# One load of a batched q k^T kernel, issued as nine partial transfers instead of one

## The chip, the core and the metric

The kernel runs on one core of a Trainium2 chip. The core has engines that run side by side, each with an instruction queue of its own: TensorE for matrix products (PE in the profile; PEld is its weight load), VectorE (DVE), ScalarE (ACT), GpSimd (POOL) and SyncE (SP), which only issues transfers and waits. Transfers between the chip's memory and the on-chip memory SBUF are done by 16 DMA engines, which ACT and SP feed through a queue each. SBUF has 128 partitions.

The metric is the device time of the program in microseconds. The time before is the median of three runs, 1063.87 us (1062.1 to 1064.1).

## The reference

```python
def setup_inputs():
    batch, n_heads, seq, head_dim = 8, 12, 1024, 64
    return {"q": ..., "k": ...}     # float32, (8, 12, 1024, 64) each

def reference(q, k):
    return np.einsum('bhid,bhjd->bhij', q, k).astype(np.float32)
```

For each of the 96 pairs of batch and head (called heads below) the scores are the 1024 x 1024 products of q's and k's rows. The inputs are 2 x 25 MB; the output is 96 x 4 MB, 403 MB.

## The kernel before

The 96 heads are grouped into nine blocks of 2, 2, 4, 8, 16, 16, 16, 16 and 16 heads (`sizes`). The first three blocks are small, so that work starts early, and block 3 (`EARLY`) is the first that is read into the input tile `x_sb`.

**Path of a block's inputs.** A block's q, and then its k, is read from memory as float32 into `x_sb`, each of the 128 partitions holding R = 8 N rows of 64 values for N heads. With 16 heads that is 8192 values, 32 KB, per partition and 4 MB in all. The method `load` does it with one transfer. `x_sb` has room for one such tensor, so a load first waits (`input_busy`) until the previous tensor has been read out. From there POOL casts it to 16 bits in pieces (`cast_quads`, line 210): a tensor of 16 heads has four pieces, each of four casts of 32 partitions. Every cast waits for the load's landing, `self.landed[x]`, which is a list of all landings of the tensor. The pieces lie in a ring of three buffers (`half`), from which DVE transposes them in 32 x 32 blocks (`transpose_quads`, line 229) into `qT` and `kT`, laid out as the products need them. Two sets of `qT` and `kT` alternate between blocks. Blocks 0 and 1 go another way, by PE's transposes.

**Scores of a head.** In `scores`, PE loads 128 columns of `qT` as weights (line 308) and multiplies with two halves of `kT` (line 311). Eight such row tiles make a head. Two of them fill half of PSUM (128 x 2048 float32), and ACT copies that half to an output tile (line 288), four copies for a head. The output tiles `o_sb` are a ring of three, 4 MB each. When a head's copies are done, SP issues one transfer of 4 MB for it (line 301); the tile is reused three heads later, when that store has landed.

**Order.** The instructions of each engine follow the order in which the program emits them. `block` runs over the heads of a block and hangs side work on them: during the heads of block i, the tensors of block i + 1 are loaded, cast and transposed. Loads are issued on ACT's queue, by `next_load(act)`, as side work of heads 1 and 7 of a block (after the copy of its second pair of row tiles): q of the next block at head 1, k at head 7. The transposes of the next block are emitted at heads 3 to 6 for q and 10 to 13 for k (`TURNS`). The last load of all is thus k of block 8 (heads 80 to 95), emitted at head 7 of block 7, head 71 of the whole.

**Landings.** A `Landing` is a semaphore that a transfer raises by 16 when it has landed. All loads of k into `x_sb` share one, and a wait names the count that it must have reached. `start` adds 16 for each transfer and returns the count up to which it has landed.

Of the kernel before, what the change touches and what calls it, by code (L numbers as in the profile page):

```python
# [8 lines left out]
P = 128  # L9
# [50 lines left out]
def kernel(  # L60
# [76 lines left out]
    class Block:  # L137
# [14 lines left out]
        def load(self, x, eng, landing=None):  # L152
            events = []
            if self.raw[x] is None:
                at = x * self.elems if self.i == EARLY else 0
                self.raw[x] = x_sb[:, at : at + self.elems]
                landing = input_landing[x]
                events = list(input_busy)
            src = flat[x][self.first * S : (self.first + self.N) * S]
            eng.wait(events)  # L160
            dma = eng.eng.dma_start(
                out=self.raw[x], in_=src.rearrange("(p r) d -> p (r d)", p=P)
            )
            self.landed[x].append(landing.start(dma))

        def load_head(self, n, x, eng, landing):
            start = (self.first + n) * S
# [156 lines left out]
    blocks, first = [], 0  # L324
# [31 lines left out]
    for x in range(2):  # L356
# [7 lines left out]
                out=ident,  # L364
                in_=ident,
# [100 lines left out]
```

## Time and profile before

| | |
|---|---|
| median of three runs | 1063.87 us (1062.1 to 1064.1) |
| profiled execution, its own time | 1062.84 us |
| its span, first to last instruction | 1061.0 us |
| TensorE clock granted | 1.0 |
| bytes moved | read 50.33 MB, written 402.65 MB |
| mean rate over the span | 427 GB/s |
| store of a head: 96 transfers on SP's queue | 4 MB each, 21.8 us from issue to landing (median) |
| load of a 16-head tensor: 10 transfers on ACT's queue | 4 MB each, 24.1 us (q) and 24.3 us (k) |
| copy of PSUM to the output tile, ACT line 288 | 384, mean 1859 ns |
| cast of 32 partitions x 2048, POOL line 210 | 176, mean 1888 ns |
| transpose, DVE line 229 | 44 of a 16- or 8-head tensor's pieces, mean 9478 and 9539 ns |

The span is the profiler's time from the first to the last instruction; the execution's own time has 1.8 us around it. Besides the engines' busy times, the profile has a record of every packet that a DMA engine moved, with its start, size and duration, and of every count by which a transfer's landing raised its semaphore: sixteen for each transfer. The packet records carry no engine number. They can be put into sixteen lanes, since on a full engine each packet begins where another ended.

A busy share of the DMA engines is the mean over the sixteen. A share slightly above 1 comes from packets that are counted whole in the window that they are assigned to.

### The profile page before, as it was taken

What the parts mean: (1) busy time and instruction counts of PE and PEld (TensorE: products, weight loads), DVE (VectorE), ACT (ScalarE), POOL (GpSimd) and SP (SyncE); (2) the same over time, 40 slices, a digit from 0 to 9 for tenths busy, and PEclk for the clock granted to TensorE, in tenths of its full rate; (3) what the DMA queues carried; (4) which work ended last, traced back from release to release, by engine and by line L of the source; (5) the groups of instructions that cost most, each with busy time, mean ns of one, the idle gap of its engine ahead of it and who ended that gap; (6) DMA issues with size and microseconds to landing.
All of it is one profiled execution on the core that took longest, in us unless ns stands there. A gap on an engine that the chain in (4) does not pass through costs nothing.

```text
span 1061.0 us, 3307 instructions
## 1 busy us (share of the span) xinstructions
PE 700.2 (66%) x1568; PEld 127.3 (12%) x800; DVE 431.0 (41%) x55; ACT 697.1 (66%) x386; POOL 354.2 (33%) x206
## 2 busy tenths in 40 slices
PE   6876744957477748567765856775584777778770
PEld 1111100111011101011111101111110111111110
DVE  2995939029193009339003907600761920000000
ACT  4766655857477747567756756775675777777771
POOL 7927465056380028064006509100913700000000
DMA  9999999999999999999999999999999999999997
GB/s 376 434 435 435 434 434 434 416 421 432 431 434 434 435 429 428 426 435 432 432 422 434 435 427 433 433 434 423 433 429 432 435 434 431 434 434 431 432 431 322
DMA packets 17009, 453.21 MB, mean 427 GB/s; under 512 B 1888, under 2 KB 1888, under 8 KB 2912
## 3 DMA queue, kind: packets, MB, share of 16 engines
q1 hardware_dynamic: 14976, 410.00, 89.7%
q10 hardware_dynamic: 2016, 42.99, 9.8%
q8 instruction: 9, 0.15, 0.0%
q14 instruction: 8, 0.07, 0.0%
HBM read 50.33 MB, written 402.65 MB: 427 GB/s over the span
## 4 chain that ended last, share of the span: by engine, by line
DMA 65%; ACT 16%; PE 7%; DVE 5%; POOL 4%; issue 1%; ACTq 0%; SPq 0%
DMA out_dram<-o_sb 60%; ACT o_sb L288 16%; PE ps_all L311 7%; DVE kT L229 4%; POOL half L210 3%; DMA x_sb<-in_k_dram 2%; DMA x_sb<-in_q_dram 2%; DVE qT L229 1%; DMA o_sb<-in_q_dram 0%; PE ps_all L243 0%; POOL qT L181 0%; DVE kT L250 0%; ACT kT L250 0%; ACTq L36 0%; SPq L169 0%
## 5 line engine op out<-in xcount | busy, mean ns | idle before, releaser
L288 ACT COPY o_sb<-ps_all 128x2048 f32<-128x2048 f32 (+1 forms) x384 | 694.8, 1859 | 333.5 <-DMA out_dram<-o_sb 290.2
L311 PE MATMUL ps_all<-kT,qT 64*128 64x512 f16 x1536 | 696.1, 617 | 328.6 <-ACT o_sb L288 312.8
L210 POOL CAST half<-x_sb 32x2048 f16<-32x2048 f32 x176 | 332.3, 1888 | 482.1 <-DMA x_sb<-in_q_dram 302.2
L229 DVE STREAM_TRANSPOSE qT<-half 128x2048 f16<-128x2048 f16 x22 | 202.6, 9478 | 268.1 <-POOL half L210 268.1
L229 DVE STREAM_TRANSPOSE kT<-half 128x2048 f16<-128x2048 f16 x22 | 202.5, 9539 | 137.5 <-POOL half L210 137.5
L308 PEld LDWEIGHTS <-qT 64*128 64x128 f16 x768 | 124.2, 162 | 897.4 <-issue 878.0
L229 DVE STREAM_TRANSPOSE kT<-kT 128x1024 f16<-128x1024 f16 x2 | 9.4, 4870 | 0.0
L229 DVE STREAM_TRANSPOSE qT<-qT 128x1024 f16<-128x1024 f16 x2 | 9.2, 4780 | 0.0
L210 POOL CAST qT<-o_sb 32x1024 f16<-32x1024 f32 x8 | 8.3, 1035 | 1.2 <-DMA o_sb<-in_q_dram 0.8
L210 POOL CAST kT<-o_sb 32x1024 f16<-32x1024 f32 x8 | 8.3, 1035 | 0.5
L250 DVE COPY qT<-ps_all 128x1024 f16<-128x1024 f16 x2 | 2.4, 1224 | 11.1 <-PE ps_all L243 11.1
L288 DVE COPY o_sb<-ps_all 128x1024 f32<-128x1024 f32 x4 | 4.9, 1225 | 4.4 <-PE ps_all L311 4.4
L243 PE MATMUL ps_all<-ident,qT 128*128 128x128 f16 x16 | 2.1, 311 | 6.8 <-POOL qT L181 6.7
L250 ACT COPY kT<-ps_all 128x1024 f16<-128x1024 f16 x1 | 1.0, 1012 | 4.8 <-PE ps_all L243 4.8
L181 POOL CAST qT<-o_sb 128x512 f16<-128x512 f32 x4 | 2.3, 615 | 3.7 <-DMA o_sb<-in_q_dram 3.7
L250 ACT ACT_TABLE_LOAD x1 | 1.3, 1283 | 2.8 <-issue 2.8
L250 DVE COPY kT<-ps_all 128x1024 f16<-128x1024 f16 x1 | 1.2, 1225 | 4.4 <-PE ps_all L243 4.4
L243 PE MATMUL ps_all<-ident,kT 128*128 128x128 f16 x16 | 2.0, 305 | 0.7 <-ACT o_sb L288 0.7
L181 POOL CAST kT<-o_sb 128x512 f16<-128x512 f32 x4 | 2.4, 618 | 0.3 <-DMA o_sb<-in_q_dram 0.3
L243 PEld LDWEIGHTS ps_all<-ident,qT 128*128 128x128 f16 x16 | 1.5, 141 | 7.1 <-POOL qT L181 7.1
L243 PEld LDWEIGHTS ps_all<-ident,kT 128*128 128x128 f16 x16 | 1.5, 136 | 3.3 <-POOL qT L210 1.6
L359 POOL MEMSET ident<- 128x128 f16 x1 | 0.2, 205 | 0.5 <-SPq L98 0.5
(5 smaller groups left out, 0.7 us busy)
## 6 DMA issues: line engine op xcount, KB each, us to landing
out_dram<-o_sb SPq DMA_DIRECT2D x96, 4096.0 KB, 21.8
x_sb<-in_q_dram ACTq DMA_DIRECT2D x5, 4096.0 KB, 24.1
x_sb<-in_k_dram ACTq DMA_DIRECT2D x5, 4096.0 KB, 24.3
x_sb<-in_q_dram SPq DMA_DIRECT2D x1, 2048.0 KB, 14.6
x_sb<-in_k_dram SPq DMA_DIRECT2D x1, 2048.0 KB, 19.5
o_sb<-in_k_dram ACTq DMA_DIRECT2D x4, 256.0 KB, 4.8
o_sb<-in_q_dram SPq DMA_DIRECT2D x4, 256.0 KB, 5.1
o_sb<-in_q_dram SPq DMA_DIRECT2D x1, 1024.0 KB, 8.2
```

The source lines that it names most:

```text
L181: lambda: nc.gpsimd.tensor_copy(out=rows[:, :, h], in_=self.raw[x][:, h * n : (h + 1) * n].rearrange("p (r d) -> p r d", d=D),),
L210: lambda: nc.gpsimd.tensor_copy(out=dst[q0 : q0 + 32].rearrange("p (r d) -> p r d", d=32), in_=raw[32 * b : 32 * b + 32, c * m : (c + 1) * ...
L229: lambda: nc.vector.transpose(out=dst, in_=buf.rearrange("p (r i) -> p r i", i=32)),
L243: lambda: nc.tensor.transpose(t_ps[:, t], rows[:, t], ident),
L250: lambda: copy(out=dst, in_=t_ps.rearrange("c t m -> c m t")), [done]
L288: lambda: (nc.vector.tensor_copy if by_dve else nc.scalar.copy)(out=dst, in_=ps[:, : w * S]),
L308: return nc.tensor.ldweights(stationary, tile_position=(at, 0))
L311: return nc.tensor.add_instruction(mybir.InstMatmult(name=nc.get_next_instruction_name(), ins=[nc.tensor.lower_ap(moving), nc.tensor.lower ...
L359: cleared = gps.run(lambda: nc.gpsimd.memset(ident, 0.0))
```

## The change

`load` issues the last load of the stream (block 8, x = 1, which is k) as nine transfers. Transfer s takes the partitions s, s + 9, s + 18, and so on: 15 partitions for s = 0 and 1, and 14 for the other seven, which together are 128. Each partition still receives its 32 KB from one contiguous stretch of memory. Each transfer raises the same semaphore by 16, and all nine counts are kept in `landed`, so that the casts wait for the last of them. Every other load is one transfer of 128 partitions, as before.

```diff
             src = flat[x][self.first * S : (self.first + self.N) * S]
+            src = src.rearrange("(p r) d -> p (r d)", p=P)
             eng.wait(events)
-            dma = eng.eng.dma_start(
-                out=self.raw[x], in_=src.rearrange("(p r) d -> p (r d)", p=P)
-            )
-            self.landed[x].append(landing.start(dma))
+            last = self.i == len(blocks) - 1 and x == 1
+            for s in range(9 if last else 1):
+                some = slice(s, P, 9) if last else slice(0, P)
+                dma = eng.eng.dma_start(out=self.raw[x][some], in_=src[some])
+                self.landed[x].append(landing.start(dma))
```

In the built program, ACT's queue has nine transfers in place of one at this point: two of 15 x 8192 and seven of 14 x 8192. The other engines' instructions and their order are the same.

## The prediction

> **What bounds the kernel now.** I read the page from the top: busy shares, the slices, the queues, the chain.
>
> ```profile
> span 1061.0 us, 3307 instructions
> ...
> PE 700.2 (66%) x1568; PEld 127.3 (12%) x800; DVE 431.0 (41%) x55; ACT 697.1 (66%) x386; POOL 354.2 (33%) x206
> ...
> DMA  9999999999999999999999999999999999999997
> GB/s 376 434 435 435 434 434 434 416 421 432 431 434 434 435 429 428 426 435 432 432 422 434 435 427 433 433 434 423 433 429 432 435 434 431 434 434 431 432 431 322
> DMA packets 17009, 453.21 MB, mean 427 GB/s; under 512 B 1888, under 2 KB 1888, under 8 KB 2912
> ...
> q1 hardware_dynamic: 14976, 410.00, 89.7%
> ...
> DMA 65%; ACT 16%; PE 7%; DVE 5%; POOL 4%; issue 1%; ACTq 0%; SPq 0%
> ```
>
> No engine is busy beyond 66%, while the sixteen DMA engines are full from the second slice to the last but one, at 434 GB/s, or 27.1 GB/s for each. The kernel is bound by the bytes it moves. The last slice, 322 GB/s, is the odd one, so I cut the end into windows. The last two columns are the busy share of the sixteen DMA engines and GB/s.
>
> ```profile
> 1052.00:1054.00 2.00, 0.00 (x0) 0.00 (x0) 0.00 (x0) 0.00 (x0) 0.00 (x0) 1.00 0.80 344
> 1054.00:1055.00 1.00, 0.00 (x0) 0.00 (x0) 0.00 (x0) 0.00 (x0) 0.00 (x0) 1.00 0.23 98
> 1055.00:1056.00 1.00, 0.00 (x0) 0.00 (x0) 0.00 (x0) 0.00 (x0) 0.00 (x0) 1.00 0.15 66
> 1056.00:1057.00 1.00, 0.00 (x0) 0.00 (x0) 0.00 (x0) 0.00 (x0) 0.00 (x0) 1.00 0.08 33
> 1057.00:1058.00 1.00, 0.00 (x0) 0.00 (x0) 0.00 (x0) 0.00 (x0) 0.00 (x0) 1.00 0.00 0
> 1058.00:1059.00 1.00, 0.00 (x0) 0.00 (x0) 0.00 (x0) 0.00 (x0) 0.00 (x0) 1.00 0.08 33
> ```
>
> A packet counts whole in one window, and 33 GB/s over 1 us is one 32 KB row. So after 1055 only four rows are left, and by 1056 a single DMA engine works alone. The trace's landing records agree: of the sixteen completions of the last store, the fourteenth comes 1.82 us after the first, the fifteenth 3.07, the sixteenth 5.94. One engine is 2.87 us behind the next. The packet records say why: a row takes 1213 ns almost always on fifteen engines and mostly 1216 to 1236 ns on one, in every stretch of the run I looked at until the last stores. That engine is not held back by a queue; it is a little slower, and the lag adds up. The chain shows the pace it sets:
>
> ```profile
> 979.68 21.71 DMA out_dram<-o_sb
> ...
> 1008.95 21.72 DMA out_dram<-o_sb
> ```
>
> Three stores take 1008.95 - 979.68 = 29.27 us by the last completion; by the first completion they take 29.04. The lag of the slow engine so grows by 0.23 per three stores. The other fifteen show no gaps between packets from about 60 us on, so none of them waits for the slow one. Each engine simply runs through its own list of rows, and the end is the longest list.
>
> **What the change does to the lists.** The q1 count above is exact for 104 transfers of 128 rows and 16 completions each (104 x 144 = 14976). So one row of a partition is one packet, and a transfer of 128 gives each engine 8. In the new load a transfer of 15 rows can occupy at most 15 engines and one of 14 rows at most 14. If each transfer is dealt out from the same first engine, which is how I read lanes that all get exactly 8 rows per transfer, then fourteen engines get 9 rows, one gets 2, one gets none. No transfer in this trace has other than 128 partitions, so that deal is not shown. The bounds are 8 rows each (if the start rotates) and 128 rows on one engine (if the rows can't be split); the 128-row transfers, dealt evenly, are nearest to one row per engine, which I take. The Trainium skill, page "DMA: Bandwidth & Descriptors", section "Why a DMA increments its semaphore by 16 and not by 1", has the largest count up to 16 that divides the outer dimension, from the lowest-numbered engine up. By it the sum would be this same one.
>
> Cost for an engine with 9 rows: one row, 1213 ns less 3.5 ns by which records overlap, is 1.21 us. Eight more completions at 9 ns, less the same overlap, are 0.05. Together 1.26 us, all on the path, since these engines are full.
>
> Gain for an engine with none: 8 x 1.21 = 9.7 us. The slow one is at most 5.94 behind the fastest, so if it is relieved it drops out of the end for good; 24 stores after the load give back only 8 x 0.23 = 1.8. With 2 rows the relief is 6 x 1.21 = 7.3, enough too against the other fourteen, which take 1.26 more.
>
> If the slow engine is relieved, the end moves to the next one: -2.87 + 1.26 = **-1.61 us**. Against the profiled execution's 1062.84 (span 1061.0 and 1.8 around it) that is 1061.2.
>
> **Issue on ACT.** One transfer becomes nine, between two copies of head 71:
>
> ```profile
> 786.85 1.87 ACT L288 COPY o_sb<-ps_all 128x2048 f32<-128x2048 f32 x1 [2.30 <-DMA out_dram<-o_sb]
> 786.90 0.33 ACTq L161 DMA_DIRECT2D x_sb<-in_k_dram  x1
> 788.62 1.87 ACT L288 COPY o_sb<-ps_all 128x2048 f32<-128x2048 f32 x1
> ```
>
> Nine at 0.33 are 3.0 us; at the pace of the first issues on SP (four in 1.82, below) 4.1. The first issue starts under the running copy, so the copy at 788.62 comes at 786.90 + 3.0 to 4.1 = 789.9 to 791.0, 1.3 to 2.4 late. Behind it stand the head's other copies, the PE halves that they free, and SP's wait for the head's store. I cost this at nothing: when a store lands and its buffer is refilled, two others are queued (2 x 9.68 = 19.4 us on an engine), the refill takes 1008.95 - 1001.47 = 7.5, so 11.9 are in hand on the slow engine and 11.9 - 5.9 = 6 on the fastest, and the load's own 9 rows add 10.9 there. Without cover it would be 2.4.
>
> **Landing of the load.** Casts on POOL wait for all nine completions.
>
> ```profile
> 0.95 1.82 SPq L169 DMA_DIRECT2D o_sb<-in_q_dram  x4
> ...
> 811.83 31.12 POOL L210 CAST half<-x_sb 32x2048 f16<-32x2048 f32 x16 [38.38 <-DMA x_sb<-in_k_dram]
> ...
> 819.59 36.80 DVE L229 STREAM_TRANSPOSE kT<-half 128x2048 f16<-128x2048 f16 x4 [32.62 <-POOL half L210]
> ```
>
> Load and store rows alternate on an engine, so the ninth row brings the landing 2 x 1.21 = 2.4 us later, plus up to 3.8 of issue. The last transpose ends at 856.4. Block 8 needs it at head 80; the copies of head 95 begin at 1030.74, fifteen heads of 29.27 / 3 earlier is 884.4, and PE starts a little before, near 880. There are 24 us to spare, so this costs nothing. POOL's wait lengthens and only DVE's transposes stand behind it.
>
> No stand-alone price for a transfer of 480 KB is in the trace. The bound from below is nothing, as lanes run from one transfer to the next with no gap; from above, the first 256 KB loads land 4.8 us after issue, of which their 16 KB per engine need 0.6 at 27.1 GB/s, so 4.2 us are latency, and eight of them 33.6. I take nothing: the gapless lanes are the nearer row, as the store ring is always full beside the load ring (the slices beside 800 us hold 431 to 434 GB/s). The Trainium skill, same page, section "Rules for kernel authors", speaks against the change: at least 1 MiB per DMA, and one 128-partition transfer rather than parts. With the page's 2.0 us fixed per transfer eight would be 16 us, an estimate. The measured fill beside the loads disagrees for this kernel.
>
> **The rivals.**
>
> *A, forecast: the slow engine is relieved.* For it: in the first transfer, which finds idle engines, the slow lane's first packet starts thirteenth or fourteenth of sixteen, so a high position is likelier than chance; against: that order is irregular. 1061.2.
>
> *B, the slow engine keeps a full list.* Then it gets 9 rows and stays last: +1.26, 1064.1, slower than before. It decides as soon as the slow engine is one of the fourteen. By counting alone it would be the rule; the starting order speaks against it. The Trainium skill, same page, section "Latency and other measured facts", calls engines 7 and 15 usually slower; 15 would be A and 7 would be B. That one engine lags agrees with the trace, which doesn't number it.
>
> *C, more than one late engine goes.* If the second-latest is the one with 2 rows, the end falls back to the fourteenth: -(5.94 - 1.82) + 1.26 = -2.86, 1060.0. The second-latest lag may also be chance: an instruction fetch of 16 KB, about 0.6 us of an engine, fell on that one at 990.
>
> *D, rows not split.* All 128 rows on one engine: 120 x 1.21 = 145 more, 1208. Against it: all 128-row transfers are split evenly.
>
> *E, the small transfers stall their lanes.* Up to 33.6 us, 1061.2 + 33.6 = 1094.8; it needs the store ring to run dry too, which it doesn't do beside any load here.
>
> *F, no effect.* The deal rotates, 8 rows each: 1062.9.
>
> **How the numbers follow.** Chances: A 0.56, C 0.12, B 0.20, D 0.03, E 0.05, F 0.04. The profiled execution is 1.03 below the median 1063.87 of the three runs (1062.1 to 1064.1), inside their range, so the lag is no artefact of profiling. The same -1.61 on the median gives 1062.3. The time will be a median of further executions, so I forecast the middle of 1061.2 and 1062.3, 1061.8. The range goes from 1059.9 (C) to 1065.2 (B on the median is 1065.1); D and E stay out. A's own range is 1060.6 to 1062.6.
>
> A measurement of this kernel can tell about 0.2%, 2.1 us, from no change, so the bounds are 1061.7 and 1066.0. A lies on the lower one: of its 0.56, 0.32 is faster and 0.24 the same. C is faster, 0.12. Of B 0.10 is the same and 0.10 slower, as its 1.3 us adds to the runs' own spread of 2. D and E are slower, F the same. Faster 0.44, same 0.38, slower 0.18.
>
> **What would show it.** In the profile after: the final windows lose the lone rows behind 1055, and the last completions lie within 2 us (A, C); three stores take 29.0 instead of 29.27 in the chain after the load; nine issues of 0.33 to 0.45 on ACT near 787; the first cast of the last load near 814 to 818, the store ring's fill unchanged. Under B the lone tail is still there, and the last completion 1.3 later. The prediction is wrong if packets of the nine transfers are spread other than 9, 2 and 0 rows, if the issues cost above 1 us each, or if rows to every ninth partition take clearly more than 1213 ns.

## The result, and the profile after

The change makes the kernel slower: 1065.09 us median (1064.04 to 1067.16, 20 runs) against 1062.53 us (1061.96 to 1064.1, 20 runs) for the kernel before, a ratio of 1.0023 with a 95% interval of 1.0017 to 1.0029. That is 2.4 us. I had forecast 1061.8 us, a small gain. The profiled execution after took 1065.03 us.

The page of the changed kernel (the busy row of the slices, the rate, the packets, the loads' queue, the chain):

```profile
span 1063.2 us, 3315 instructions
...
DMA  9999999999999999999999999999999999999997
GB/s 375 433 434 434 434 431 432 428 423 433 431 433 433 434 415 432 434 434 433 433 431 434 430 423 431 434 434 432 434 428 401 433 430 433 431 433 431 431 431 313
DMA packets 17121, 453.21 MB, mean 426 GB/s; under 512 B 2000, under 2 KB 2000, under 8 KB 3024
...
q10 hardware_dynamic: 2128, 42.99, 9.7%
...
DMA 64%; ACT 16%; PE 7%; DVE 5%; POOL 4%; ACTq 1%; issue 1%; SPq 0%
```

Four things differ. ACT's queue has entered the chain (ACTq 1%, before 0%). The packets below 512 B are the completions: 112 more than the 1888 of before. One transfer of 16 completions has become nine, and 2 x 15 + 7 x 14 - 16 = 112, so a transfer of 15 partitions ran on 15 engines and one of 14 on 14, as assumed. The Trainium skill, page "DMA: Bandwidth & Descriptors", section "Why a DMA increments its semaphore by 16 and not by 1", says the same of how many engines are used, and the trace agrees. The slice with 401 GB/s, the thirty-first, is the stretch of the changed load; before, no slice between the first and the last was below 416. And the last slice has not become fuller (313 against 322).

The end in windows (last columns: busy share of the DMA engines, GB/s):

```profile
1054.00:1055.00 1.00, 0.00 (x0) 0.00 (x0) 0.00 (x0) 0.00 (x0) 0.00 (x0) 1.00 0.53 229
1055.00:1056.00 1.00, 0.00 (x0) 0.00 (x0) 0.00 (x0) 0.00 (x0) 0.00 (x0) 1.00 0.38 164
1056.00:1057.00 1.00, 0.00 (x0) 0.00 (x0) 0.00 (x0) 0.00 (x0) 0.00 (x0) 1.00 0.30 131
1057.00:1058.00 1.00, 0.00 (x0) 0.00 (x0) 0.00 (x0) 0.00 (x0) 0.00 (x0) 1.00 0.15 66
1058.00:1059.00 1.00, 0.00 (x0) 0.00 (x0) 0.00 (x0) 0.00 (x0) 0.00 (x0) 1.00 0.00 0
1059.00:1060.00 1.00, 0.00 (x0) 0.00 (x0) 0.00 (x0) 0.00 (x0) 0.00 (x0) 1.00 0.08 33
1060.00:1061.00 1.00, 0.00 (x0) 0.00 (x0) 0.00 (x0) 0.00 (x0) 0.00 (x0) 1.00 0.08 33
```

The lone tail is still there, moved to later. From the landing records: the last store's sixteenth completion comes 6.76 us after the first, and 2.82 after the fifteenth (before: 5.94 and 2.87). The lagging engine was not relieved.

The chain says where the time was lost. Its pieces "DMA out_dram<-o_sb" end when a store lands, and one piece stands for three stores (columns: start, duration). Before:

```profile
765.01 21.77 DMA out_dram<-o_sb
...
794.33 31.41 DMA out_dram<-o_sb
...
833.30 21.73 DMA out_dram<-o_sb
...
862.59 21.71 DMA out_dram<-o_sb
```

After:

```profile
765.09 21.78 DMA out_dram<-o_sb
...
805.94 21.97 DMA out_dram<-o_sb
...
835.46 21.77 DMA out_dram<-o_sb
...
864.78 21.72 DMA out_dram<-o_sb
```

The landing of head 68's store is at 786.78 before (765.01 + 21.77) and 786.87 after. The landing three stores later is at 825.74 before and 827.91 after: the step with the load takes 38.96 us before and 41.04 after, 2.08 more. The next but one step is 29.27 (833.30 + 21.73 to 862.59 + 21.71) before and 29.27 after (835.46 + 21.77 to 864.78 + 21.72): the slow engine's pace, not the 29.0 that I expected. All of the loss is made at the load and kept to the end. In the landing records the way from head 68's last completion to the last of all is 272.97 us before and 275.09 after. I use this figure for the experiments too, as "way to the end"; it leaves out what differs between executions before the load.

ACT around the load, after:

```profile
786.94 1.86 ACT L290 COPY o_sb<-ps_all 128x2048 f32<-128x2048 f32 x1 [2.33 <-DMA out_dram<-o_sb]
786.99 2.30 ACTq L165 DMA_DIRECT2D x_sb<-in_k_dram  x2
788.71 1.87 ACT L290 COPY o_sb<-ps_all 128x2048 f32<-128x2048 f32 x1
789.32 12.91 ACTq L165 DMA_DIRECT2D x_sb<-in_k_dram  x7
802.28 3.63 ACT L290 COPY o_sb<-ps_all 128x2048 f32<-128x2048 f32 x2 [11.70 <-issue]
```

The nine issues took 2.30 + 12.91 = 15.2 us, 1.7 each, where I had 3.0 to 4.1 in all, and head 71's third copy came at 802.28 instead of 790.67. The landing was later too (first cast and first transpose of the tensor, after):

```profile
824.32 31.09 POOL L212 CAST half<-x_sb 32x2048 f16<-32x2048 f32 x16 [51.16 <-DMA x_sb<-in_k_dram]
...
832.08 36.75 DVE L231 STREAM_TRANSPOSE kT<-half 128x2048 f16<-128x2048 f16 x4 [45.41 <-POOL half L212]
```

The first cast moved from 811.83 to 824.32. The last transpose ends at 868.8, still before the 880 at which block 8 needs it.

So three candidates for the 2.1 to 2.4 us stood beside each other: the ninth row on the slow engine (theory L, lists), ACT held for 15 us (theory I, issues), and packets that are slowed because of where the rows land (theory S, stretch). In the packet records after, store packets between 797 and 840 on the record's clock (which runs 11 us ahead of the span's, so about 786 to 829) are 24.1 us longer in sum than 1213 ns each, against 1.2 before; on the engine that ends last, two store packets took 1461 and 1968 ns.

### The profile page after: what moved, and what is told of

The parts are those of the page before. It is cut to its first block, busy times and chain, and to the rows that moved or that the text cites. A ratio compares the mean times of both kernels' runs of the same rounds, so it can differ in the third digit from the quotient of the medians.

```text
span 1063.2 us, 3315 instructions
## 1 busy us (share of the span) xinstructions
PE 700.6 (66%) x1568; PEld 127.4 (12%) x800; DVE 430.9 (41%) x55; ACT 697.2 (66%) x386; POOL 354.0 (33%) x206
## 4 chain that ended last, share of the span: by engine, by line
DMA 64%; ACT 16%; PE 7%; DVE 5%; POOL 4%; ACTq 1%; issue 1%; SPq 0%
DMA out_dram<-o_sb 59%; ACT o_sb L290 16%; PE ps_all L313 7%; DVE kT L231 4%; POOL half L212 3%; DMA x_sb<-in_k_dram 2%; DMA x_sb<-in_q_dram 2%; ACTq L165 1%; DVE qT L231 1%; DMA o_sb<-in_q_dram 0%; PE ps_all L245 0%; POOL qT L183 0%; DVE kT L252 0%; ACT kT L252 0%; ACTq L36 0%
```

## The experiments

Every edit is in `load`, if not said otherwise, and is shown against the line `some = slice(s, P, 9)` of the change; the computation is unaltered in all. The time is the ratio to the kernel before on the same chip with its interval; 0.1% is 1.06 us. The way to the end is from one profiled execution each, and that one can lie off the median: with every eighth partition, and with 112, 8 and 8, it was the fastest of five.

| | ratio, 95% interval | way to the end, above before |
|---|---|---|
| the change | 1.0023, 1.0017 to 1.0029 | +2.12 us |
| the change again | 1.0022, 1.0013 to 1.0031 | +1.97 |
| 8 transfers of 16, every eighth | 1.0035, 1.0022 to 1.0047 | +1.80 |
| 126 and 2 neighbours | 1.0016, 1.0007 to 1.0025 | +1.22 |
| 120 and 8 neighbours | 1.0071, 1.0058 to 1.0083 | +8.33 |
| 112, 8 and 8 neighbours | 1.0048, 1.0035 to 1.0062 | +4.06 |
| the ninth transfer as 7 and 7 | 1.0038, 1.0025 to 1.0051 | +3.36 |
| the ninth transfer as 8 and 6 | 1.0031, 1.0019 to 1.0042 | +3.50 |
| whole load, 8 tiny transfers behind it | 1.0002, 0.9994 to 1.0011 | +0.61 |
| whole load, 24 tiny transfers | 1.0011, 1.0002 to 1.0020 | +0.73 |
| nine transfers of neighbours | 1.0114, 1.0097 to 1.0130 | +10.80 |
| 8 transfers of 16, every seventh | 1.0043, 1.0030 to 1.0056 | +4.13 |
| nine transfers, issues spread out | 1.0019, 1.0010 to 1.0028 | +1.88 |
| 126 and 2, with 16 tiny transfers | 1.0017, 1.0007 to 1.0026 | +1.66 |
| an eighth of the load by GpSimd | 1.0003, 0.9995 to 1.0012 | -0.64 |

**Even deal, many issues.**

```diff
-            for s in range(9 if last else 1):
-                some = slice(s, P, 9) if last else slice(0, P)
+            for some in [slice(s, P, 8) for s in range(8)] if last else [slice(0, P)]:
```

> The last load as eight transfers of 16 partitions (every eighth), so that each DMA engine should get 8 rows as before, with eight issues. Theory L (lists: the slow engine got a ninth row, and the end follows its list): no ninth row, so 0 to +0.3 us against before, whatever the issues take. Theory I (the issues: nine took 2.30 + 12.91 = 15.2 us of ACT's queue, and the late store of head 71 leaves engines without rows): +1.0 to +1.5 us, if issues of 16 partitions take 1.7 us each too. If they take 0.33 us each, it is 14 and 15 partitions that are slow to issue, and theory I expects 0. Theory S (rows to scattered partitions stretch, up to 2.25 us in the profile of the change): +0.5 to +1.5 us, with row records well above 1213 ns.

Measured: +0.35%, a median above the change's. Each engine has 8 rows here, so theory L alone (0 to 0.3 us) falls. The issues took 11.7 us of ACT. Of the 128 load packets 77 were above 1250 ns, with a mean of 1394. Theory S is seen at work; theory I isn't excluded by this run.

**Uneven deal, two issues.** `[slice(0, 126), slice(126, P)]`

> The last load as two transfers, of 126 and 2 neighbouring partitions. The uneven deal nearly without the issues: 9 rows on fourteen engines, none on two, and one more row on the first two. Theory L: +1.2 us against before (+2.4 if the slow engine is one of the first two). Theory I: two issues cost ACT nothing, so whatever of the +2.5 us of the change was due to issues is gone; if theory I were all of it, 0. Theory S: neighbouring partitions as before, no stretched rows, so the remainder of +1.3 us is gone.

Measured: +0.16% (1.7 us, 0.7 to 2.7), a way of +1.22. This is the ninth row (1.21 us), with no nine issues and load packets of 1261 ns on average, as before (1252). Store packets became longer here too, by 15.2 us in sum, but none on the engine that ends last. It is below the change in the way, 1.22 against 2.12; the two intervals of the times overlap.

**Where the slow engine stands.** `[slice(0, 120), slice(120, P)]` and `[slice(0, 112), slice(112, 120), slice(120, P)]`

> The last load as transfers of 120 and 8 partitions: 9 rows on the first eight engines, 8 on the next seven, none on the last. It asks where the slow engine stands. Theory L: +1.2 us if it is one of the first eight, 0 if one of the next seven, -1.5 us if it is the last (the end then moves to the next engine). Theories I and S: 0, as there are two issues and neighbouring partitions.

> The last load as transfers of 112, 8 and 8 partitions: 9 rows on the first eight engines, 7 on the other eight. Theory L: +1.2 us if the slow engine is one of the first eight, -1.2 us if one of the other eight. Theories I and S: 0.

Both missed by far: +0.71% and +0.48%. The deal was as meant (completions 15 + 8 and 16 + 8 + 8, by the count of small packets, 1895 and 1904). But load packets took 1807 and 1455 ns on average; of the 128, 120 and 68 were above 1250. The rate around the load in the run with 120 and 8 (windows, last columns busy share and GB/s):

```profile
790.00:800.00 10.00, 5.86 (x14) 0.95 (x7) 0.00 (x0) 3.96 (x3) 0.00 (x0) 1.00 1.04 328
800.00:810.00 10.00, 2.02 (x5) 0.32 (x2) 0.00 (x0) 3.76 (x3) 0.00 (x0) 1.00 0.99 351
810.00:820.00 10.00, 5.23 (x12) 0.97 (x6) 0.00 (x0) 3.51 (x2) 0.00 (x0) 1.00 1.00 367
```

The engines are busy all the time and move a fifth less: packets are slow, not missing. What the runs still say about the slow engine: with 120 and 8, one engine got no row of this load, and the last engine of the kernel still lagged, 5.4 us behind the next. So the engine that was left out isn't the slow one. Which of the others it is can't be read from these two, because the stretch is larger than a row.

**Splitting the ninth transfer.** The eight transfers of every ninth partition, then `[slice(8, 71, 9), slice(71, P, 9)]` or `[slice(8, 80, 9), slice(80, P, 9)]`; the change itself ran beside them.

> The change itself once more, beside the next two on one chip. +2.4 to +2.6 us against before, as on the first chip. In the trace the last completion of the last engine should move by about 2 us between the stores just before and just after the load, and by nothing later.

> The change with its ninth transfer of 14 partitions split into two of 7, ten transfers in all. If 7 partitions go to the first seven engines, these get 10 rows and the next seven 8. Theory L with the slow engine the eighth: -1.2 us against the change (one row less on it). Theory L with the slow engine among the first seven: +1.2 us against the change. Theory L with it among the ninth to fourteenth: -1.2 us as well, but the transfers of 112, 8 and 8 partitions then should not have lengthened its list. Theory I (issues): +0.2 us for one issue more.

> The same with the ninth transfer split into 8 and 6: the first six engines get 10 rows, the seventh and eighth 9, the next six 8. With the slow engine the eighth or the seventh: 0 against the change, so 1.2 us above the split into 7 and 7 if it is the eighth. With it among the first six: +1.2. With it among the ninth to fourteenth: -1.2.

Measured: the change again +0.22%; the splits +0.38% and +0.31%, 2.3 and 1.7 us above the change's median. The ways are 1.2 and 1.4 above the change's. That is the direction for a slow engine among the first six, which gets a tenth row in both; among the seventh to fourteenth it would be 0 or a gain in one of them. The intervals of the times overlap with the change's, and the split of 7 and 7 was off by twice the row; so the times make the place likely and don't settle it. The packet records say more: followed back, the engine that ends last has ten rows of the load with 7 and 7 (table below), so it is among those that the transfers of 7 use. With 8 and 6 it has ten too, with two doubtful links. In the repeat of the change, another engine was the last at the load (its step there is 42.14) and the slow one caught up with it by the end, where the two are 0.41 us apart; the way to the end is the same within 0.2 us.

**The issues alone.** The kernel before, and behind its whole last load:

```diff
+                for s in range(8):
+                    tiny = eng.eng.dma_start(
+                        out=scratch[0:14, s : s + 1], in_=kk[0:14, s : s + 1]
+                    )
```

> The kernel before with its whole last load of 128 partitions, and behind it on ACT's queue eight transfers of 14 partitions by one value (4 bytes) into a scratch tile: the issues without the deal. Theory I: if they take 1.5 us each as in the change, ACT is held 12 us and the end comes 0.8 to 1.4 us later. Theories L and S: 0 (within 0.4 us), as the rows and where they land are those of before.

> Twenty-four transfers of 14 values behind the whole last load, where eight held ACT for 7.8 us and cost nothing. At the same 0.9 us each ACT is held 22 us, longer than the 15.2 us of the change. If ACT's hold is covered by the stores and the load that are queued: 0 to +0.5 us. If the cover ends below 15 us (theory I): +1 us or more, with gaps in the lanes.

ACT with eight and with twenty-four tiny transfers:

```profile
787.56 0.33 ACTq L163 DMA_DIRECT2D x_sb<-in_k_dram  x1
787.92 1.50 ACTq L170 DMA_DIRECT2D scratch<-in_k_dram  x1
...
789.45 6.26 ACTq L170 DMA_DIRECT2D scratch<-in_k_dram  x7
795.74 3.63 ACT L297 COPY o_sb<-ps_all 128x2048 f32<-128x2048 f32 x2 [4.60 <-issue]
```

```profile
789.19 17.18 ACTq L170 DMA_DIRECT2D scratch<-in_k_dram  x23
806.41 3.64 ACT L297 COPY o_sb<-ps_all 128x2048 f32<-128x2048 f32 x2 [15.57 <-issue]
```

A hold of 7.8 us (1.50 + 6.26) costs nothing that can be measured. One of 18.7 (1.54 for the first, 17.18 for the rest) costs 0.11%, at the edge of the measurement. Eleven packets of the late store took 3.3 to 4.5 us there, but at every moment from 797 to 850 on the record's clock at least sixteen packets were under way, so the records show no engine that ran dry. Whether the cover ends between the two, where the change's 15.2 us lies, they don't tell; further below the hold is taken from the change, and added to another deal.

**Only which partitions go together.** The change with neighbouring partitions in each transfer, `[slice(0, 15), slice(15, 30), *(slice(s, s + 14) for s in range(30, P, 14))]`.

> The change with the same nine transfers of 15, 15 and seven times 14 partitions, but of neighbouring partitions instead of every ninth: the deal of rows to engines and the issues stay, only where the rows land changes. Theory S (a transfer's rows that land in neighbouring partitions hold each other up, as the 120 of neighbours did with rows of 1807 ns on average): at least 3 us slower than the change, with load rows well above 1213 ns. Theory L alone: the change's +2.4 us, unaltered.

Measured: +1.14%, 12 us; load packets of 2078 ns on average, 115 above 1250. The deal and the number of issues are the change's, and the issues were shorter (2.07 + 4.32 = 6.4 us). Rate around the load:

```profile
790.00:800.00 10.00, 7.10 (x16) 1.27 (x8) 0.00 (x0) 5.37 (x3) 0.00 (x0) 1.00 1.05 288
800.00:810.00 10.00, 0.64 (x3) 0.10 (x1) 0.00 (x0) 2.40 (x2) 0.00 (x0) 1.00 1.02 347
810.00:820.00 10.00, 6.78 (x16) 1.20 (x8) 0.00 (x0) 4.88 (x3) 0.00 (x0) 1.00 0.92 338
```

and of the change itself, and of before:

```profile
790.00:800.00 10.00, 2.49 (x6) 0.47 (x3) 0.00 (x0) 0.58 (x1) 0.00 (x0) 1.00 1.00 413
800.00:810.00 10.00, 5.62 (x13) 0.97 (x6) 0.00 (x0) 7.37 (x5) 0.00 (x0) 1.00 0.97 383
810.00:820.00 10.00, 8.11 (x19) 1.46 (x9) 0.00 (x0) 8.11 (x5) 0.00 (x0) 1.00 0.97 393
```

```profile
790.00:800.00 10.00, 6.03 (x14) 1.11 (x7) 0.00 (x0) 4.12 (x3) 0.00 (x0) 1.00 1.02 426
800.00:810.00 10.00, 5.28 (x12) 0.98 (x6) 0.00 (x0) 7.21 (x4) 0.00 (x0) 1.00 1.00 433
810.00:820.00 10.00, 4.04 (x10) 0.65 (x4) 0.41 (x1) 3.87 (x4) 7.93 (x5) 1.00 0.99 429
```

Which partitions a transfer covers decides how fast its packets are. Every ninth partition avoids most of it, but not all. A partition's place in SBUF and its row in memory change together in all these runs, so whether it is where rows land (theory S) or where they are read from was not told apart.

**Even deal, every seventh.** `[*(slice(s, 112, 7) for s in range(7)), slice(112, P)]`

> Eight transfers of 16 partitions (seven of every seventh partition, one of the last sixteen): an even deal of 8 rows each, so no ninth row, with rows spread out more than by every eighth. Theory L: what stands above before is then not the ninth row. Theory S: stretched rows alone, +0.8 to +2 us, in any case less than the +3.7 us with every eighth partition; the last engine's time over the three stores around the load exceeds that of before by what its rows are stretched.

Measured: +0.43%, not below the run with every eighth: a miss of that bound. Load packets of 1511 ns on average. It confirms that an even deal is no help if the packets stretch.

**The hold taken away, and added.** First, the change with three issues left in their place and three pairs as side work later; the casts wait for all nine as before.

```diff
+            for some in parts[:3]:
+                issue(some)
+            later.extend(lambda some=some: issue(some) for some in parts[3:])
...
+            if i == len(blocks) - 2 and n in (7, 8):
+                for u in (3,) if n == 7 else (1, 3):
+                    side[u] = side.get(u, []) + [
+                        lambda: [later.pop(0)() for _ in range(2)]
+                    ]
```

> The change with its nine issues put in four places on ACT's queue, three after the second copy of head 71, then two each after its fourth, and after the second and fourth of head 72. ACT is held some 5 us at most in one place instead of 15. If what the change costs beyond the ninth row (1.26 of 2.4 us) is the hold, it comes to +1.2 to +1.5 us against before; if it is rows that stretch each other, it stays at +2.2 to +2.6.

Second, the load as 126 and 2 with sixteen tiny transfers behind it.

> The load as 126 and 2 neighbouring partitions (ninth row on fourteen engines, +1.7 us alone), with sixteen transfers of 14 values behind it, which at 0.75 to 0.9 us hold ACT about 14 us. If a hold of 15 us costs nothing: +1.2 to +1.8 us, as without them. If the hold is the rest of the change's cost: +2.2 to +2.8.

Measured: without the hold +0.19% (0.10 to 0.28) and a way of +1.88, so most of the cost stays. The 2.0 us lie between the two forecasts, nearer to "rows that stretch" than to "the hold", whose bound of 1.2 to 1.5 us the interval does not exclude (0.10% is 1.1 us). Its load packets were of 1221 ns, but the store packets beside them were 29.0 us longer in sum, as in the change (24.1). With 126 and 2, ACT held for 13.3 us (1.19 + 12.06) added 0.01%, from 1.0016 to 1.0017. Both make it likely that the hold is little of it.

**The last engine, packet by packet.** The packets of the engine that ends last can be followed back from a last completion, each to the one that ended where it began; where two fit, the one is taken that leaves eight store rows to a completion. In these runs the chain has no gap above 22 ns around the load, and no load row on it is more than 20 ns above 1213. The sums are over its store packets from 785 to 860 on the record's clock.

| | rows of the load | store packets above 1213 ns, sum | way to the end, above before |
|---|---|---|---|
| before | 8 | 0.52 us | |
| the change | 9 | 1.34 | +2.12 us |
| the change again | 9 | 1.22 | +1.97 |
| 126 and 2 neighbours | 9 | 0.49 | +1.22 |
| nine transfers, issues spread out | 9 | 1.12 | +1.88 |
| 126 and 2, with 16 tiny transfers | 9 | 0.79 | +1.66 |
| the ninth transfer as 7 and 7 | 10 | 1.38 | +3.36 |

The change's 2.12 us are the ninth row with its completions, 1.26, and 0.82 of longer store packets (1.34 - 0.52). The engine had no time in which it waited, so ACT's hold did not reach it as a wait. The tenth row adds 1.2. Why store packets on it became longer stays open.

**From the other side.** Seven eighths of the load's columns in one transfer of 128 partitions, the rest issued by GpSimd in two, each behind a transfer of 8 values.

```diff
+            n = self.elems * 7 // 8 if last else self.elems
+            dma = eng.eng.dma_start(out=self.raw[x][:, :n], in_=src[:, :n])
...
+                    tiny = nc.gpsimd.dma_start(
+                        out=scratch[0:8, j : j + 1], in_=src[0:8, j : j + 1]
+                    )
...
+                    dma = nc.gpsimd.dma_start(
+                        out=self.raw[x][some, n:], in_=src[some, n:]
+                    )
```

> An attempt at a faster version: seven eighths of the columns of the last load as one transfer of 128 partitions; the last eighth issued by GpSimd as transfers of 120 and 8 partitions, each behind one of 8 values that should move GpSimd's choice of engines on by eight. If the two large ones then go to the upper eight engines, the lower eight have one row's worth (1.21 us) less, the slow one among them: theory L expects -1.0 to -1.3 us. If GpSimd deals them in another way, 0 to +1.

Measured: +0.03% (-0.05 to +0.12), no gain. Followed back in the same way, the engine that ends last has eight rows of 28 KB and nine of 4 KB of this load: GpSimd's transfers went to it too, so it was not relieved. The way to the end is 0.64 us shorter in its one profile, but most of the 4 KB rows ran before head 68's last completion, from which the way is counted, so that is no gain. No version that beats the kernel before was found.

## Why the prediction was wrong, step by step

- *The bound.* Right. The sixteen DMA engines are full, and the end is the longest list of one lagging engine; in the repeats too the loss arose at the load and was carried to the end unaltered.
- *The deal: 9 rows on fourteen engines, 2 and 0 on two.* Right as far as it can be seen: the 112 further completions show on how many engines each transfer ran, and the engine that ends last has nine rows.
- *"If the slow engine is relieved."* This is the step that failed. I gave 0.56 + 0.12 to the cases in which it is, because its first packet started late in the first transfer. It kept a full list and got the ninth row: its packets hold nine rows of the load, the steps of the chain after the load stay at 29.27, and the last completion stays 2.82 behind the next. So instead of -1.61 the sum had to start from +1.26. The order of first packets was no evidence. By counting alone, fourteen of sixteen, rival B was the likelier, and it was what happened. The Trainium skill, page "DMA: Bandwidth & Descriptors", section "Latency and other measured facts", names engines 7 and 15 as usually slower. By its order of dealing, from the lowest engine up, the one without rows is 15, and the runs show that this isn't the slow one here; by the same order the split of 7 and 7 gives a tenth row to engines 0 to 6 alone, and as the slow one has ten, it isn't 7 either.
- *Cost of the ninth row, 1.26 us.* Right in size: 126 and 2 neighbours, the uneven deal without the rest, has a way of +1.22.
- *Rival B's sum, 1064.1 on the execution's own 1062.84, +1.26.* Too small. The change cost 2.4 us. What was missing is that packets become longer: I had it as a sign of error ("clearly more than 1213 ns"), with no price. Load packets stayed at 1262 ns on average (before 1252), but store packets beside them became longer. On the engine that ends last two were longer by 248 and 755 ns, and all of them together by 0.8 us more than before, which with 1.26 comes to 2.1 of the 2.12 in the profiled execution. That the measured 1065.09 still lies below the forecast's upper end, 1065.2, is luck: that end was 1.26 on the median of three runs, 1063.87, and twenty runs give 1062.53.
- *Issue on ACT, 3.0 to 4.1 us, at no cost.* The size was off by four: 15.2 us. That it is covered holds: the engine that ends last never waited, 13.3 us held cost nothing measurable beside the same deal, and spreading the issues gained at most little. The end of the cover, which I had at 11.9 us, was not found: 13.3 us still cost nothing measurable, and 18.7 cost 0.11% (0.02 to 0.20).
- *Landing, 814 to 818.* 824.32, with longer issues and longer packets, which were not told apart here; hidden as said, with 868.8 for the last transpose.
- *Small transfers stall their lanes (rival E).* Not seen; eight tiny transfers cost nothing.

## What to carry to other kernels

Where the DMA engines are the bound, a load is a list of packets for each engine: before it is dealt out unevenly, know which engine ends last, and don't take a hint for that knowledge, since an extra row on it is paid in full (here 1.2 us). A transfer's choice of partitions sets the speed of its packets: one transfer of all 128 gave 1252 ns per row, parts of the same load between 1221 and 2078. And price an issue from one of the same form: 0.33 us for 128 partitions said nothing of the 1.7 us for 14 of every ninth.

## What the runs showed that I had not expected

- One DMA engine is slower in every profile here (packets mostly of 1216 to 1236 ns instead of 1213), from the first 40 us on, and it comes last by 2.8 us at the end of both kernels (by 0.4 in the repeat of the change).
- An issue of a transfer of every ninth partition took ACT 1.7 us (1.3 where the nine were spread out, 11.4 in sum), of 14 neighbours 0.7 (2.07 for three, 4.32 for six), of 128 partitions 0.33.
- Rows to neighbouring partitions in transfers of 14 or 15 took 2078 ns each, in one of 120 1807, in one of 126 1261, with all 128 at once 1252. Why the number matters so much stays open.
- Engines that a load leaves out don't keep their lead. By the lists, the two lightest engines of the change come out of the load 10.9 and 8.5 us ahead of the fourteen (nine and seven rows of 1.21). In the landing records of head 71's store, the first two completions are only 2.4 and 1.6 us ahead of the middle one. Between lie longer store packets (24.1 us in sum over all engines) and 4.1 us, also in sum, in which engines had no packet (797 to 850 on the record's clock); the two lanes themselves can't be followed for certain.
